# A two-block transformer on one core: four weight splits on another engine, and three steps added to the order of the second block

## The chip, the cores and the metric

The kernel runs on one core of a Trainium2 chip. The metric is the device time of one execution in microseconds (us), from the first to the last instruction with what lies around them; smaller is better. The engines are TensorE (PE in the rows; its weight loads are PEld), VectorE (DVE), ScalarE (ACT), GpSimd (POOL) and SyncE (SP, which issues most DMAs). Each engine works through its own queue in order; semaphores tie the queues together.

## What is computed

512 tokens of width 1024 go through two blocks, one layer each, all in 32-bit floats. The first block (a retention mixer, an RWKV mixer, cross-attention to 256 memory rows, a squared-ReLU MLP) is not touched by the change. The second block, which is, is this, cut to what matters:

```python
h = rmsnorm_2(x, norm_gain)
z = h @ w_in                                   # 1024 -> 4864
q, k, v, gate_a, u_in, v_in, gate_b, g_merge = split(z)
q = axial_rope(rmsnorm_2(q.reshape(B, S, 8, 64), q_gain), row_ang, col_ang)
k = axial_rope(rmsnorm_2(k.reshape(B, S, 2, 64), k_gain), row_ang, col_ang)
attn = block_attention(q, k, v) * silu(gate_a)   # 8 query heads, 2 key heads
y_a = attn @ w_proj_attn
u = gelu(u_in)
vv = layernorm(gelu(v_in), ln_v_gain, ln_v_bias)
v_mix = einsum('gij,bcjgd->bcigd', w_spatial, vv) + b_spatial
y_b = (u * v_mix * silu(gate_b)) @ w_proj_gmlp
g = sigmoid(g_merge + b_merge)
y = g[0] * y_a + g[1] * y_b
out = rmsnorm_2(x + y @ w_out, final_gain)
```

## The kernel before

**Weights.** All large weights lie in one stream of 189 units of 128 x 1024 floats, taken in order. A unit is loaded by SP into `raw`, rounded to the TensorE's reduced float form on ScalarE (`wh`, line 295), and the rest that the rounding lost is a subtraction `raw - wh` (`wl`, line 296). Each product of two matrices is then three TensorE products: high x high, high x low, low x high. Every fourth unit uses buffers of its own, named `rawx`, `whx`, `wlx` in the rows; the three others rotate over three buffers, so the cast of unit 148 can only start when the products with unit 144 are done. `self.lowpart(u)` says on which engine the subtraction of unit u runs: GpSimd where it is true, VectorE where not. Units are split three ahead of their use (`pump`).

**Units of the second block** (counted from the order of packing): 135 to 138 are q, 139 and 140 are k and v, 141 to 144 are u_in (one tile of 24 products each), 145 to 148 are v_in (one group of 96 products, which walks through all four units for each of the four row blocks), 149 to 156 the two gates, 157 to 172 the merge gates (16 tiles of 24 products), 173 to 188 the projections and the output.

**Order.** The order of the program is written out by hand with generators. `streams` runs a main generator one step at a time; each step issues about four large products. After each step it runs those side generators whose time has come: a `yield n` in a side generator means "go on n steps later". The TensorE's order is exactly the order of issue; the other engines' queues are ordered by the scheduler of the framework. Side generators here:
- `heads(b)` (lines 1229 to 1277): norm and rotation of q and k for row block b. The inverse root is `power` (line 372), a GpSimd operation; VectorE then scales (1244), multiplies by the rotation tables (1248), GpSimd adds the halves (1252, 1253), TensorE transposes, ScalarE and VectorE split the result (1261, 1262).
- `layer_norm(b)` (1298 to 1312): statistics on VectorE, `power` on GpSimd, scaling on VectorE (1307, 1308), gain and bias on GpSimd (1309, 1310).
- `attention()` (1365 to 1394): for each of 8 heads, four blocks of scores (`score`, into PSUM `tp`, softmax at lines 1109 to 1114) and four `turn`s (transposes of the probabilities into PSUM `ch`, split by ScalarE line 896 and VectorE line 897), then the products with the values: 8 products in two halves of four. They take the high and the low part of the turned probabilities in turn, so the second of them already needs the last VectorE split of the last `turn`.

Attention runs as a side stream between the products of the 16 merge-gate tiles. GELU (1194 to 1197) uses both ScalarE and VectorE. At the start of each tile ScalarE casts a unit (295) and evicts the tile before (1418), and GpSimd or VectorE makes a low part.

In the rows, `mm` and `cs` are the PSUM tiles of the main products; `s` and `t` are activations and temporaries. I number attention heads from 0, as the code does.

Of the kernel before, what the change touches and what calls it, by code (L numbers as in the profile page):

```python
# [212 lines left out]
class Ordered:  # L213


    def __init__(self, tc, eng):
        self.tc, self.eng, self.last = tc, eng, None
# [12 lines left out]
class Kern:  # L230
    def __init__(self, ctx, tc, A, out):
        self.tc, self.nc, self.A, self.out = tc, tc.nc, A, out
        self.T = Ordered(tc, tc.nc.tensor)
        pool = lambda name, **k: ctx.enter_context(tc.tile_pool(name=name, bufs=1, **k))
        self.cp = pool("cp")
        self.wp = pool("wp")
        self.tp = pool("tp")
        self.sp = pool("sp")
        self.sm = pool("sm")
        self.dp = pool("dp", space=bass.MemoryType.DRAM)  # L240
        self.nraw = self.nspl = 0
        self.raw, self.spl = {}, {}
        self.NU = A["wst"].shape[0]
        self.u = 0
        self.cnt = 0
        self.nh = 3
        self.lowpart = lambda u: u <= 3 or 55 <= u < 79 or 145 <= u
        self.wait = [40, 16]


# [948 lines left out]
    def second(self):  # L1199
# [32 lines left out]
        def heads(b):  # L1232
            x = qk[b]
            x3 = x.rearrange("p (h d) -> p h d", d=64)
            sq = self.tmp((P, 640), "t4", 2)
            for i in range(2):
                for k in range(2):
                    G.tensor_tensor(tab[i][k][:, b], tb[:, k, b], gq[i], op=ALU.mult)  # L1238
            SC.activation(sq, x, AF.Square)
            ss = self.small(10)  # L1240
            V.tensor_reduce(ss, sq.rearrange("p (h d) -> p h d", d=64), axis=AX.X, op=ALU.add)
            V.tensor_scalar(ss, ss, 1.0 / 64, 1e-6, op0=ALU.mult, op1=ALU.add)
            rn = self.power(ss, 10)
            V.tensor_tensor(x3, x3, rn.unsqueeze(2).broadcast_to([P, 10, 64]), op=ALU.mult)
            aa, bb = self.tmp((P, 640), "t4", 2), self.tmp((P, 640), "t4", 2)
            for i, (h0, h1) in enumerate(((0, 8), (8, 10))):
                for k, o in ((0, aa), (1, bb)):
                    V.tensor_tensor(o.rearrange("p (h d) -> p h d", d=64)[:, h0:h1], x3[:, h0:h1],
                                    tab[i][k][:, b].unsqueeze(1).broadcast_to([P, h1 - h0, 64]), op=ALU.mult)
            yield 3  # L1250
            v5 = lambda t: t.rearrange("p (g a f) -> p g a f", a=2, f=16)
            G.tensor_tensor(v5(x)[:, :, 0], v5(aa)[:, :, 0], v5(bb)[:, :, 1], op=ALU.subtract)
            G.tensor_tensor(v5(x)[:, :, 1], v5(aa)[:, :, 1], v5(bb)[:, :, 0], op=ALU.add)
            yield 15
            c = slice(b * 128, b * 128 + 128)
            tr = self.psum("tp", (P, 4, 128))
            for i in range(4):
                self.T.transpose(tr[:, i], x[:, i * 128:i * 128 + 128], self.ident)

            for q, (o, w) in zip(qt, both):  # L1260
                SC.copy(q[o, :, c], tr[o])
                V.tensor_tensor(q[w, :, c], tr[o], q[o, :, c].bitcast(F32), op=ALU.subtract)
            if b < NB - 1:
                return

            t = self.tmp((P, 2, 512), "t4", 2, F32R)
            kl.extend(t[:, r] for r in range(2))
            tr = self.psum("tp", (P, 4, 128))
            for i in range(NB):
                self.T.transpose(tr[:, i], qk[i][:, 512:640], self.ident)  # L1270
            tr = tr.rearrange("p a b -> p (a b)")
            for k, l, (o, w) in zip(kh, kl, both):
                SC.copy(k[o], tr[o])
                SC.copy(k[w], tr[o])
                V.tensor_tensor(l[o], tr[o], k[o].bitcast(F32), op=ALU.subtract)
                V.tensor_tensor(l[w], tr[o], k[o].bitcast(F32), op=ALU.subtract)
            self.flags.add("keys")
# [3 lines left out]
        def post(b, ps):  # L1281
            SC.copy(qk[b][:, 512:640], ps[:, 0:128])
            c = slice(b * 128, b * 128 + 64)
            self.psplit((vh[:, :, c], vl[:, :, c]), ps[:, 128:256].rearrange("p (r d) -> p r d", d=64))
            self.spawn(heads(b), 9 * b)
# [8 lines left out]
        def post(b, ps):  # L1294
            self.gelu2(ps, v2[:, b])
            self.spawn(layer_norm(b), 8)

        def layer_norm(b):
            v = v2[:, b]
            st = self.small(6)  # L1300
            V.bn_stats(st, v)
            mv = self.small(2)
            V.bn_aggr(mv, st)
            e = self.small(1)
            V.tensor_scalar(e, mv[:, 1:2], 0.25, 1e-6, op0=ALU.mult, op1=ALU.add)
            rs = self.power(e, 1)
            V.tensor_scalar(rs, rs, 0.5, None, op0=ALU.mult)
            V.tensor_scalar(v, v, mv[:, 0:1], rs, op0=ALU.subtract, op1=ALU.mult)
            G.tensor_tensor(v, v, lnt[:, 0], op=ALU.mult)
            G.tensor_tensor(v, v, lnt[:, 1], op=ALU.add)  # L1310
            return
            yield

        yield from self.quad(lambda k: h2[k], post, outer=True)

# [33 lines left out]
        def score(i):  # L1349
            p, r = i // 8, i // 4 % 2  # L1350
            c = slice(i % 4 * 128, i % 4 * 128 + 128)
            sc = self.psum("tp")
            self.T.matmul(sc, qt[r][:, p, c], kh[r], start=True, stop=False)
            self.T.matmul(sc, qt[r][:, p, c], kl[r], start=False, stop=True)
            pr[i] = self.softmax(sc, 512, 0.125)

        def turn(i):
            c = slice(i % 4 * 128, i % 4 * 128 + 128)
            if i % 4 == 0:
                pts[i // 4] = self.slab(13, [P, 4, 512], F32R), self.slab(17, [P, 4, 512], F32R)  # L1360
            pt = pts[i // 4]
            tr = self.psum("ch", (P, 4, 128))
            for m in range(4):
                self.T.transpose(tr[:, m], pr[i][:, m * 128:m * 128 + 128], self.ident)
            self.psplit((pt[0][:, :, c], pt[1][:, :, c]), tr)

        def attention():
            score(0)
            yield 1
            score(1)  # L1370
            yield 1
            for i in range(32):
                if i + 2 < 32:
                    score(i + 2)
                    yield 1
                turn(i)
                yield 1
                if i % 4 == 3:
                    hd = i // 4
                    o, w = both[hd % 2]  # L1380
                    yield 1
                    ps = self.psum("ch")
                    for m in range(4):
                        for k in range(2):
                            self.T.matmul(ps, vs(hd % 2, m), pts[hd][k][:, m], start=m + k == 0, stop=m + k == 4)
                        if m == 1:
                            yield 1
                    g = sga[o, hd // 2]
                    lo = self.tmp()
                    SC.activation(lo[o], ps[w], AF.Copy)  # L1390
                    V.tensor_tensor(lo[o], ps[o], lo[o], op=ALU.add)
                    V.scalar_tensor_tensor(g, lo[o], 0.5, g, op0=ALU.mult, op1=ALU.mult)
                    yield 1
            self.flags.add("attention")
# [16 lines left out]
        def post_b(j, ps):  # L1411
            o = th[2 + j // 4][:, j % 4]
            V.scalar_tensor_tensor(o, o, 1.0, ps, op0=ALU.add, op1=ALU.mult)

        self.spawn(attention(), 1)
        for j in range(16):
            ps = yield from self.tile_t(h2)
# [345 lines left out]
```

## Time and profile before

| | |
|---|---|
| time, median of 3 runs | 1276.71 us (1273.4 to 1277.31) |
| the profiled execution's own time | 1280.32 us |
| its span, first to last instruction | 1278.6 us |
| mean granted TensorE clock | 0.988 of full |
| TensorE busy | 1244.9 us, 97% of the span |
| VectorE busy | 654.0 us, 51% |
| ScalarE busy | 508.8 us, 40% |
| GpSimd busy | 473.0 us, 37% |

The busy time of TensorE comes from modelled ends of its matmuls, so a short wait can hide in it; the time from one matmul's start to the next one's start shows it better. Back-to-back products of 512 columns start about 0.23 us apart in this kernel. The granted clock is 1.0 at 2.4 GHz and 0.5 at 1.2 GHz.

### The profile page before, as it was taken

The page shows a single profiled execution, that of the slowest core. Times are in us where ns is not written, and L with a number is a line of the kernel's source. Part 1 is how long each engine was busy: PE and PEld are TensorE (multiplying, and loading weights), DVE is VectorE, ACT ScalarE, POOL GpSimd, SP SyncE. Part 2 cuts the span into 40 slices and gives each one's busy share as a digit, 9 for nine tenths or more (in the row PEclk, how much of TensorE's full clock was granted, in tenths as well). Part 3 has the DMA queues.
Part 4 walks back from the last instruction along what each step waited for, and adds up shares of the span by engine and source line. Part 5 has one row for each costly group of instructions (what it writes and reads, how often), then busy time and mean ns, then how long its engine had stood idle before and what let it go on. Part 6 is the DMA issues. An engine that isn't in the chain of part 4 may idle for free.

```text
span 1278.6 us, 17927 instructions
## 1 busy us (share of the span) xinstructions
PE 1244.9 (97%) x6976; PEld 1030.4 (81%) x6976; DVE 654.0 (51%) x1239; ACT 508.8 (40%) x919; POOL 473.0 (37%) x512
## 2 busy tenths in 40 slices
PE   7999989999999999999999999999999999999997
PEld 5777779887987888798888888888787878787886
DVE  4777334566784455434333333334667456564353
ACT  5434244232354444444332232234444445455232
POOL 4927571353200332344110111012526843233475
PEclk9999899999999999999999999999999999999999
DMA  5222423121345222223233333243232322121321
GB/s 202 74 67 85 114 51 86 50 67 34 117 138 178 78 86 66 83 81 118 88 95 98 99 99 97 92 119 97 93 103 63 116 83 66 50 67 50 115 83 67
DMA packets 52087, 115.47 MB, mean 90 GB/s; under 512 B 23169, under 2 KB 23809, under 8 KB 52002
## 3 DMA queue, kind: packets, MB, share of 16 engines
q1 hardware_dynamic: 47600, 113.73, 29.4%
q8 instruction: 55, 0.90, 0.3%
q10 hardware_dynamic: 4370, 0.59, 0.3%
q14 instruction: 30, 0.25, 0.1%
q0 software_dynamic: 32, 0.00, 0.0%
HBM read 110.90 MB, written 3.41 MB: 89 GB/s over the span
## 4 chain that ended last, share of the span: by engine, by line
PE 85%; DVE 5%; POOL 4%; ACT 3%; DMA 1%; issue 1%; ACTq 0%; POOLq 0%; DVEq 0%; SPq 0%
PE mm L221 40%; PE cs L221 33%; PE ch L221 8%; PE tp L221 4%; POOL o L1640 1%; POOL s L1642 1%; ACT wh L295 1%; DVE wl L296 1%; POOL s L1238 1%; ACT t L1112 0%; DVE t L1114 0%; DVE st L1718 0%; DVE s L221 0%; DVE s L897 0%; DMA s<-dm 0%
## 5 line engine op out<-in xcount | busy, mean ns | idle before, releaser
L221 PE MATMUL mm<-s,wh 128*128 128x512 f32 (+1 forms) x880 | 263.6, 379 | 2.3 <-DVE kt L775 2.1
L295 ACT CAST wh<-raw 128x1024 fp32r<-128x1024 f32 x151 | 158.7, 1051 | 259.7 <-PE mm L221 179.5
L221 PE MATMUL mm<-wh,s 128*128 128x512 f32 (+1 forms) x824 | 233.6, 352 | 3.8 <-DVE t L729 2.0
L296 DVE TENSOR_TENSOR wl<-raw,wh 128x1024 fp32r<-128x1024 f32 x99 | 122.9, 1241 | 156.3 <-ACT wh L295 155.9
L221 PEld LDWEIGHTS mm<-s,wh 128*128 128x128 f32 x880 | 159.6, 190 | 36.8 <-issue 6.2
L296 POOL TENSOR_TENSOR wl<-raw,wh 128x1024 fp32r<-128x1024 f32 x52 | 125.9, 2424 | 142.8 <-ACT wh L295 131.6
L221 PEld LDWEIGHTS mm<-wh,s 128*128 128x128 f32 x824 | 148.7, 194 | 24.3 <-issue 2.9
L221 PE MATMUL mm<-s,wl 128*128 128x512 f32 (+1 forms) x432 | 163.2, 378 | 1.0 <-DVE wl L221 1.0
L221 PE MATMUL cs<-s,wh 128*128 128x512 f32 (+1 forms) x544 | 154.8, 368 | 0.0
L221 PE MATMUL mm<-wl,s 128*128 128x512 f32 (+1 forms) x412 | 141.9, 344 | 2.1 <-POOL wl L296 1.6
L221 PE MATMUL cs<-wh,s 128*128 128x512 f32 (+1 forms) x440 | 142.2, 387 | 0.0
L1130 POOL TENSOR_TENSOR t<-t 128x512 f32<-128x512 f32 x32 | 49.9, 1558 | 217.0 <-ACT t L1129 217.0
L221 PEld LDWEIGHTS cs<-s,wh 128*128 128x128 f32 x544 | 98.2, 190 | 16.4 <-issue 0.2
L221 PE MATMUL cs<-s,wl 128*128 128x512 f32 (+1 forms) x272 | 99.9, 367 | 0.0
L221 PEld LDWEIGHTS cs<-wh,s 128*128 128x128 f32 x440 | 81.8, 188 | 16.4
L221 PEld LDWEIGHTS mm<-s,wl 128*128 128x128 f32 x432 | 82.4, 191 | 14.5 <-DVE wl L221 1.2
L296 POOL TENSOR_TENSOR wlx<-raw,whx 128x1024 fp32r<-128x1024 f32 x17 | 41.3, 2427 | 139.8 <-ACT whx L295 136.6
L221 PEld LDWEIGHTS mm<-wl,s 128*128 128x128 f32 x412 | 80.2, 195 | 11.7 <-POOL wl L296 2.0
L221 PE MATMUL cs<-wl,s 128*128 128x512 f32 (+1 forms) x220 | 85.1, 387 | 0.0
L351 DVE TENSOR_TENSOR s<-t,s 128x512 fp32r<-128x512 f32 x44 | 34.7, 790 | 65.2 <-ACT s L350 65.2
L221 PE MATMUL ch<-s,s 128*64 128x64 f32 (+3 forms) x504 | 62.5, 272 | 4.9 <-ACT s L1702 2.4
L295 ACT CAST whx<-raw 128x1024 fp32r<-128x1024 f32 x35 | 36.7, 1047 | 72.6 <-PE mm L221 53.0
(312 smaller groups left out, 2095.2 us busy)
## 6 DMA issues: line engine op xcount, KB each, us to landing
raw<-wst SPq DMA_DIRECT2D x189, 512.0 KB, 3.6
s<-x SPq DMA_DIRECT2D x8, 512.0 KB, 5.0
s<-rows SPq DMA_DIRECT2D x4, 512.0 KB, 4.0
out<-t SPq DMA_DIRECT2D x8, 256.0 KB, 2.2
t<-mem SPq DMA_DIRECT2D x2, 512.0 KB, 4.6
dm<-s ACTq DMA_DIRECT2D x8, 64.0 KB, 1.9
s<-dm SPq DMA_DIRECT2D x2, 256.0 KB, 4.1
s<-dm SPq DMA_DIRECT2D x8, 64.0 KB, 2.9
```

The costliest lines, as they stand in the source:

```text
L221: r = getattr(self.eng, name)(*a, **k)
L295: (SC or nc.scalar).copy(h, r)
L296: (E or (nc.gpsimd if self.lowpart(self.nspl) else nc.vector)).tensor_tensor(l, r, h.bitcast(F32), op=ALU.subtract)
L351: self.nc.vector.tensor_tensor(dst[1], src, dst[0].bitcast(F32), op=ALU.subtract)
L1130: nc.gpsimd.tensor_tensor(q, r, r, op=ALU.mult)
L1238: G.tensor_tensor(tab[i][k][:, b], tb[:, k, b], gq[i], op=ALU.mult)
L1640: G.tensor_tensor(tv, w[:, 0:k, s:s + 1].broadcast_to([P, k, n]), m[:, s:s + 1, s + 1:32].broadcast_to([P, k, n]), op=ALU.mult)
L1642: G.tensor_tensor(w[:, 0:k, s + 1:32], w[:, 0:k, s + 1:32], tv, op=ALU.add)
```

## The change

Three edits, all in the second block. Units 145 to 148 (v_in) get their low parts on VectorE instead of GpSimd. In `heads` and in `layer_norm` a `yield 2` stands between the power operation and the first instruction that uses its result, so that what follows is issued two steps later (in `heads` the transposes too, since the later waits count from there). In `attention` the pause between the last `turn` of a head and its value products is two steps instead of one.

```diff
-        self.lowpart = lambda u: u <= 3 or 55 <= u < 79 or 145 <= u
+        self.lowpart = lambda u: u <= 3 or 55 <= u < 79 or 149 <= u
...
             rn = self.power(ss, 10)
+            yield 2
             V.tensor_tensor(x3, x3, rn.unsqueeze(2).broadcast_to([P, 10, 64]), op=ALU.mult)
...
             rs = self.power(e, 1)
+            yield 2
             V.tensor_scalar(rs, rs, 0.5, None, op0=ALU.mult)
             V.tensor_scalar(v, v, mv[:, 0:1], rs, op0=ALU.subtract, op1=ALU.mult)
             G.tensor_tensor(v, v, lnt[:, 0], op=ALU.mult)
             G.tensor_tensor(v, v, lnt[:, 1], op=ALU.add)
-            return
-            yield
...
                 if i % 4 == 3:
                     hd = i // 4
                     o, w = both[hd % 2]
-                    yield 1
+                    yield 2
                     ps = self.psum("ch")
```

The instructions are the same but for their engine: VectorE has four more, GpSimd four fewer. Lines after 1243 have numbers one higher in the changed kernel up to `layer_norm`, and the old numbers again after it.

**ScalarE, around the cast of unit 148 (`wh_8737`), before.** Line 1261 splits turned q, 1239 squares for the norm, 1194 and 1196 are GELU of a tile of u_in.

```order
L1261 CAST s_1379_8169<-tp_8703 64x4x128
L1196 ACTIVATE t_8683<-t_8682 128x512
L1261 CAST s_1380_8170<-tp_8703 64x4x128
L1239 ACTIVATE t_1479_8750<-s_1378_8168 128x640
L295 CAST wh_8737<-raw_8631 128x1024
L1194 ACTIVATE t_8728<-mm_8694 128x512
```

The same place in the changed kernel:

```order
L1262 CAST s_1379_8169<-tp_8711 64x4x128
L295 CAST wh_8737<-raw_8631 128x1024
L1194 ACTIVATE t_8728<-mm_8692 128x512
L1262 CAST s_1380_8170<-tp_8711 64x4x128
L1239 ACTIVATE t_1479_8750<-s_1378_8168 128x640
L1196 ACTIVATE t_8729<-t_8728 128x512
```

The cast of unit 148 has moved ahead of a GELU step (1196), the second q split and the square; before, it stood behind all of them.

**VectorE, the same stretch, before.** 1244 scales q and k by the root, 1248 are the four rotation products, 1195 and 1197 belong to GELU.

```order
L1195 SCALAR_TENSOR_TENSOR t_8625<-t_8625,cs_8591 128x512
L1242 TENSOR_SCALAR sm_8652<-sm_8652 128x10
L1197 SCALAR_TENSOR_TENSOR s_1434_8521<-t_8626,cs_8591 128x512
L1244 TENSOR_TENSOR s_1378_8168<-s_1378_8168,sm_8655 128x640
L1248 TENSOR_TENSOR t_1463_8658<-s_1378_8168,s_1373_8149 128x512
L1248 TENSOR_TENSOR t_1464_8659<-s_1378_8168,s_1373_8149 128x512
L1248 TENSOR_TENSOR t_1463_8658<-s_1378_8168,s_1373_8149 128x128
L1248 TENSOR_TENSOR t_1464_8659<-s_1378_8168,s_1373_8149 128x128
L1195 SCALAR_TENSOR_TENSOR t_8682<-t_8682,cs_8637 128x512
L1262 TENSOR_TENSOR s_1379_8169<-tp_8703,s_1379_8169 64x4x128
L1197 SCALAR_TENSOR_TENSOR s_1434_8521<-t_8683,cs_8637 128x512
L1262 TENSOR_TENSOR s_1380_8170<-tp_8703,s_1380_8170 64x4x128
```

In the changed kernel (`wlx_8689` is the low part of unit 147, `wl_8738` that of unit 148):

```order
L296 TENSOR_TENSOR wlx_8689<-raw_8583,whx_8688 128x1024
L1195 SCALAR_TENSOR_TENSOR t_8680<-t_8680,cs_8637 128x512
L1245 TENSOR_TENSOR s_1378_8168<-s_1378_8168,sm_8655 128x640
L1197 SCALAR_TENSOR_TENSOR s_1434_8521<-t_8681,cs_8637 128x512
L1249 TENSOR_TENSOR t_1463_8666<-s_1378_8168,s_1373_8149 128x512
L1249 TENSOR_TENSOR t_1464_8667<-s_1378_8168,s_1373_8149 128x512
L1249 TENSOR_TENSOR t_1463_8666<-s_1378_8168,s_1373_8149 128x128
L1249 TENSOR_TENSOR t_1464_8667<-s_1378_8168,s_1373_8149 128x128
L1263 TENSOR_TENSOR s_1379_8169<-tp_8711,s_1379_8169 64x4x128
L296 TENSOR_TENSOR wl_8738<-raw_8631,wh_8737 128x1024
L1195 SCALAR_TENSOR_TENSOR t_8728<-t_8728,mm_8692 128x512
L1263 TENSOR_TENSOR s_1380_8170<-tp_8711,s_1380_8170 64x4x128
```

Two of the four new subtractions are seen here. The scaling (now 1245) has moved ahead of a GELU step, and the low part of unit 148 stands behind the four rotation products and one q split.

**TensorE, from the last turn of head 2 (the transposes with `ident`) to the first of its value products (`ch` from two `s`), before:**

```order
L221 MATMUL ch_9757<-ident,t_9689 128x128 x4
L221 MATMUL cs_9741<-s_1287_7754,wh_9490 128x512
L221 MATMUL cs_9741<-s_1285_7752,wl_9491 128x512
L221 MATMUL cs_9741<-s_1285_7752,wh_9490 128x512
L221 MATMUL cs_9741<-s_1287_7754,wh_9490 128x512
L221 MATMUL cs_9741<-s_1285_7752,wl_9491 128x512
L221 MATMUL cs_9741<-s_1285_7752,wh_9490 128x512
L221 MATMUL cs_9741<-s_1287_7754,wh_9490 128x512
L221 MATMUL cs_9741<-s_1285_7752,wl_9491 128x512
L221 MATMUL ch_9772<-s_1660_9669,s_1381_8171 128x512
```

In the changed kernel:

```order
L221 MATMUL ch_9765<-ident,t_9697 128x128 x4
L221 MATMUL cs_9723<-s_1286_7753,wh_9485 128x512
L221 MATMUL cs_9723<-s_1288_7755,wh_9485 128x512
L221 MATMUL cs_9723<-s_1286_7753,wl_9486 128x512
L221 MATMUL cs_9723<-s_1286_7753,wh_9485 128x512
...
L221 MATMUL cs_9723<-s_1286_7753,wl_9486 128x512
L221 MATMUL cs_9723<-s_1286_7753,wh_9485 128x512
L221 MATMUL cs_9723<-s_1288_7755,wh_9485 128x512
L221 MATMUL cs_9723<-s_1286_7753,wl_9486 128x512
L221 MATMUL ch_9792<-s_1660_9677,s_1381_8171 128x512
```

Eight main products stood between the turn and the value products; now there are twelve (four of them are the rows left out). The same holds for all eight heads: a head now takes 12 steps, 48 main products, which is two tiles, where it took 11 steps and 44 products (the last head, with no more scores to make, takes 40 where it took 36). So the tiles' starts fall at the same place of every head: counted from a head's value products, its successor's turns stand 12, 20, 28 and 36 products later and its value products 48 later, at the end of a tile. Before, this drifted by four products per head; only head 5's value products stood at the end of a tile (after 264 of the 384 products), and head 6's turns followed it 12, 20, 28 and 36 products later, its value products 44 later.

## Rows read from the trace of the kernel before

**Rows 1.** The page: busy time of an engine, share of the span, instructions.
```profile
PE 1244.9 (97%) x6976; PEld 1030.4 (81%) x6976; DVE 654.0 (51%) x1239; ACT 508.8 (40%) x919; POOL 473.0 (37%) x512
```

**Rows 2.** Busy time by stretch: each engine's, then granted clock, DMA share, GB/s.
```profile
1080.00:1100.00 20.00, 18.21 (x80) 14.27 (x79) 12.26 (x24) 8.23 (x17) 4.79 (x2) 0.91 0.19 53
1100.00:1180.00 80.00, 79.37 (x381) 63.65 (x380) 45.24 (x103) 42.50 (x81) 22.13 (x10) 1.00 0.20 60
...
1094.00:1098.00 4.00, 4.00 (x11) 3.14 (x12) 0.00 (x0) 0.00 (x0) 0.00 (x0) 0.57 0.37 123
```

**Rows 3.** Instructions in time (start, length, engine, line): TensorE at unit 148.
```profile
971.05 0.39 PE L221 MATMUL mm<-s,wl 128*128 128x512 f32 x1
...
975.39 0.40 PE L221 MATMUL mm<-wh,s 128*128 128x512 f32 x1
977.40 0.50 PE L221 MATMUL mm<-wl,s 128*128 128x512 f32 x1 [1.61 <-POOL wl L296]
```

**Rows 4.** The same view, other engines, on the way to unit 148's low part.
```profile
965.33 1.05 ACT L295 CAST whx<-raw 128x1024 fp32r<-128x1024 f32 x1 [0.52 <-PE cs L221]
...
966.47 2.39 POOL L296 TENSOR_TENSOR wlx<-raw,whx 128x1024 fp32r<-128x1024 f32 x1
966.54 3.00 DVE L1244 TENSOR_TENSOR s<-s,sm 128x640 f32<-128x640 f32 x1 [1.00 <-POOL sm L372]
...
969.58 1.70 DVE L1248 TENSOR_TENSOR t<-s,s 128x512 f32<-128x512 f32 x4
...
971.90 0.63 ACT L1196 ACTIVATE t<-t 128x512 f32<-128x512 f32 x1 [3.54 <-DVE t L1195]
...
973.87 1.03 ACT L295 CAST wh<-raw 128x1024 fp32r<-128x1024 f32 x1
...
974.98 2.36 POOL L296 TENSOR_TENSOR wl<-raw,wh 128x1024 fp32r<-128x1024 f32 x1 [1.91 <-ACT wh L295]
```

**Rows 5.** The page's costliest groups: a low part made on VectorE.
```profile
L296 DVE TENSOR_TENSOR wl<-raw,wh 128x1024 fp32r<-128x1024 f32 x99 | 122.9, 1241 | 156.3 <-ACT wh L295 155.9
```

**Rows 6.** Instructions in time: a VectorE low part beside GpSimd's rotation.
```profile
947.99 0.88 POOL L1253 TENSOR_TENSOR s<-t,t 128x320 f32<-128x320 f32 x1
948.20 1.75 DVE L296 TENSOR_TENSOR wlx<-raw,whx 128x1024 fp32r<-128x1024 f32 x1 [1.00 <-ACT whx L295]
```

**Rows 7.** Instructions in time, TensorE: value products of head 2.
```profile
1091.19 0.39 PE L221 MATMUL cs<-s,wl 128*128 128x512 f32 x1
1092.24 0.49 PE L221 MATMUL ch<-s,s 128*128 128x512 f32 x1 [0.66 <-ACT s L896]
1093.87 1.21 PE L221 MATMUL ch<-s,s 128*128 128x512 f32 x3 [1.13 <-DVE s L897]
...
1098.08 0.39 PE L221 MATMUL cs<-s,wh 128*128 128x512 f32 x1
```

**Rows 8.** The same time on the other engines.
```profile
1090.53 2.39 POOL L296 TENSOR_TENSOR wl<-raw,wh 128x1024 fp32r<-128x1024 f32 x1 [7.53 <-ACT wh L295]
...
1091.94 1.27 DVE L1114 TENSOR_SCALAR t<-t,sm 128x512 f32<-128x512 f32 x1
...
1093.13 0.68 DVE L897 TENSOR_TENSOR s<-ch,s 128x512 fp32r<-128x512 f32 x1
```

**Rows 9.** Instructions in time, TensorE: value products of head 4.
```profile
1127.41 0.40 PE L221 MATMUL ch<-s,s 128*128 128x512 f32 x1
1127.98 0.96 PE L221 MATMUL ch<-s,s 128*128 128x512 f32 x3 [0.17 <-DVE s L897]
```

**Rows 10.** Instructions in time: head 5's value products, and the end of head 6.
```profile
1143.55 1.09 PE L221 MATMUL ch<-s,s 128*128 128x512 f32 x4
...
1154.17 2.41 POOL L296 TENSOR_TENSOR wl<-raw,wh 128x1024 fp32r<-128x1024 f32 x1 [7.09 <-ACT wh L295]
...
1158.82 0.68 DVE L897 TENSOR_TENSOR s<-ch,s 128x512 fp32r<-128x512 f32 x1
...
1159.25 1.28 PE L221 MATMUL ch<-s,s 128*128 128x512 f32 x4
```

## The prediction

> **What bounds the kernel now.** I read the page first, then busy time by stretch, then the order of instructions in time, engine by engine. TensorE is busy for 97% of the span [rows 1], so nothing that only shortens work on another engine can show; a gain must be time in which TensorE stood still or ran at half clock. In the page the reader should compare the shares, and then look for stretches where TensorE falls short of their length. In the second block there are few: it stands still for 1.79 us of 1080 to 1100 and for 0.63 us of the 80 us after it [rows 2], and once in the v_in products, at unit 148 [rows 3]. Within 1094 to 1098 the mean granted clock is 0.57, so nearly all of it ran at the lower of the two levels, 1.2 GHz [rows 2]. That is all that the change can win, since it touches nothing ahead of 940 us and moves no TensorE work.
>
> Because a wait can hide in a modelled end, I size each by the time between two starts less the regular 0.23 us.
>
> **Unit 148 (the low parts on VectorE).** From 975.39 to 977.40 TensorE waits for unit 148's low part: 2.01 - 0.23 = 1.8 us [rows 3]. The rows tell how it came to be late. GpSimd makes unit 147's low part from 966.47 on; VectorE's scaling of k and q, issued just behind it, takes 3.00 us until 969.54, right after GpSimd ends; a GELU step on ScalarE then waits 3.54 us for VectorE, and behind it in ScalarE's queue stands the cast of unit 148 (973.87), though the buffer had been free since the last product with unit 144 at 971.4; the low part then takes 2.36 us on GpSimd [rows 3, 4].
>
> After the change nothing long of GpSimd's stands in the way of the scaling. The cast stands behind one q split only and can run from 971.4, when the buffer is free, to 972.4. On VectorE I add up what stands ahead of unit 148 from the end of unit 147's cast, 966.4 [rows 4]: that unit's low part 1.24 [rows 5], two GELU steps and one q split of 0.7 each (estimated from a split of that width, 0.68 [rows 8]), the scaling 0.8 (an estimate: 3.00 us less the 2.2 in which GpSimd was at work), the rotations 1.70 [rows 4]. That is 5.8 us, so VectorE is free at 972.2; the low part starts with the cast's end and is done at 972.4 + 1.24 = 973.6. TensorE asks for it at 975.39 + 0.23 = 975.6: 2.0 us to spare. Against this, GpSimd's two rotation sums of 0.88 us each start just then, when the rotations are done, and a VectorE low part that began beside such a sum took 1.75 us instead of 1.24 [rows 6]. If both sums hold it up it ends near 972.4 + 1.76 + 1.24 = 975.4, still 0.2 us early. If VectorE besides ran 1 us late, TensorE would wait 0.8. So the term lies between 1.0 and 1.8; I take **1.8**, as only two things together would cost any of it.
>
> The trace shows one engine standing until the other is done. The Trainium skill has this as a rule ("SBUF — State Buffer", section "Who interferes with whom"): a VectorE instruction with two SBUF inputs contends with a GpSimd one that reads SBUF, and the order of issue decides who stands still. The 3.00 us and the 1.75 us agree with it [rows 4, 6]. The rule speaks against this edit: it lets the power operation as well hold up a VectorE low part, which these rows don't show. If it does so for unit 147, by the 1.00 us that the scaling waited for that power, and the sums then hold up unit 148, both things do come together: the term is 1.0 by the rule, the sum 6.2 and the time 1270.5 instead of 1269.7.
>
> The four subtractions cost VectorE 4 x 1.24 = 5 us; it is idle for half of the span [rows 1], and what they delay (GELU, rotation of later row blocks) has several microseconds until TensorE asks. They take 4 x 2.4 us from GpSimd, which nobody waits for there but VectorE. Cost to the end: **0**. If that cover were gone, the q and k transposes would be late; they are issued eight products (1.8 us) later than before.
>
> **The steps after the power operation.** They add no instruction. They let VectorE take other work while GpSimd is at the power; that only shortens VectorE's waits. Bounds: nothing won beyond unit 148's term above, where the reordering is already counted, and at most 1 us lost if a transposed block came late. I take **0**.
>
> **The value products one step later.** What TensorE waits for there is the split of the last turn. The extra step puts four more main products, 4 x 0.23 = 0.92 us, between turn and value products; their work is not new, it only comes earlier. The terms:
> - Head 2, waits: 1091.19 to 1092.24 and 1092.24 to 1093.87, less 0.23 each: 0.82 + 1.40 = **2.2 us** [rows 7].
> - Head 2, clock: from 1093.87 to 1098.08 eleven products start, which at the regular 0.23 would be 2.53 us; they took 4.21, so **1.7 us** [rows 7]. The granted clock is 0.57 there and 1.0 in the stretch after it [rows 2]; the drop follows right on the two waits. It would go with them. Whether each execution has it I can't see from one; bounds 0 and 1.7.
> - Heads 3 to 7, waits: 0.63 us of idle [rows 2] is the lower bound. For head 4 the start-to-start time gives 0.57 - 0.23 = 0.34 where 0.17 is shown as idle [rows 9], so twice the idle, 1.3, is likelier; I take **1.3**.
>
> Do 0.92 us do? For head 2 alone they would not: its split ends at 1093.81, and with four more products TensorE would ask at about 1092.7. But the phase moves too. Head 2 was late because a tile's start fell into its last softmax: the unit cast there brought a GpSimd low part (1090.53 + 2.39 = 1092.92), and the last softmax scaling on VectorE took 1.27 us, until just after that, with the split behind it [rows 8]. After the change every head has the phase that heads 5 and 6 had before: value products at a tile's end, turns 12, 20, 28 and 36 products on. So the stretch from 1143.55 to 1159.25 is what each later head will look like, with four products more at its end [rows 10]. In it GpSimd's low part ends at 1156.6, well before the last split, and that split ends at 1158.82 + 0.68 = 1159.50, where TensorE asked for it at 1159.25 + 0.23 = 1159.48. With 0.92 us more that leaves 0.9 us to spare, seven times over. This is why I count all of the attention's waits as gone.
>
> At the other end, attention runs on for 32 products longer, into the first third of the next projection; 100 main products, 23 us, still lie between it and the projection that needs it. Cost: **0**.
>
> **Sum.** 1.8 + 2.2 + 1.7 + 1.3 = 7.0 us, against the profiled execution's 1280.32 us (span 1278.6): 1273.3 for such an execution. The median of the runs is 1276.71, 3.6 us lower, and I take the same difference off it: 1276.71 - 7.0 = **1269.7 us**.
>
> **Rivals.**
> 1. Only half of it shows. Unprofiled runs have no drop in the clock to win back, and either unit 148 is still late or the waits of heads 3 to 7 stay. For it: one profiled execution is all that shows the drop, and the sum on VectorE has 0.2 us to spare in its worse case. The gain is then 1.0 + 2.2 = 3.2 us or less: about 1273.5.
> 2. The change does nothing that can be told: TensorE's waits come back elsewhere in the stretch, as VectorE, held up by GpSimd, frees PSUM buffers later. For it: VectorE is at work for 45 and GpSimd for 22 of the 80 us after 1100. Against: TensorE stands still there for 0.63 us only, though that stretch has heads in four different phases [rows 2]. 1276 us.
> 3. Slower: the fixed phase is a bad one. If GpSimd's low part came to end beside the last softmax scaling of every head, each would lose head 2's 2.2 us less the 0.9 to spare, seven times: 9 us, against 7.0 won, so 1279; with a drop in the clock at each (7 x 1.7) up to 1291. In head 2 GpSimd was done 0.2 us before the split began (1092.92 and 1093.13), in the phase to come 2.2 us before it (1156.58 and 1158.82) [rows 8, 10]. It decides from the point where a cast comes some 2 us later than in rows 10, and the order of ScalarE's queue there gives no reason for that.
>
> **Chances.** Forecast (gains of 4 to 8 us) 0.74; rival 1 0.13; rival 2 0.09; rival 3 0.04. 0.3% of the median is 3.8 us, about what a measurement of this kernel can tell from no change. Forecast falls on the faster side; of rival 1 I put 0.03 there too: faster 0.77. Same 0.10 + 0.09 = 0.19, slower 0.04 (rival 3). The range: the lowest run of before less the whole sum is 1273.4 - 7.0 = 1266.4, and with a microsecond for waits sized too small 1265.4; upward it takes in most of rival 1, up to 1275.0. The forecast's own range is 1266.4 to 1272.7.
>
> **What would show it.** In the changed kernel: no wait of TensorE for a low part near 975 us, and the cast of unit 148 near 971; TensorE's start-to-start times at value products all near 0.23 us; a granted clock of 1.0 from 1080 to 1100; the attention's heads about 16 us apart. It is wrong if value products of all heads wait for line 897, if TensorE waits for a VectorE low part in v_in, or if a new half-clock stretch appears after 940 us.

## The result, and the profile after

The changed kernel takes 1271.07 us (median of 6 runs, 1267.94 to 1271.63); the kernel before, run beside it, 1277.6 us (6 runs, 1273.4 to 1280.13). The ratio is 0.9937 with a 95% interval of 0.9918 to 0.9955: faster, by 0.6%. The forecast was 1269.7 us (1265.4 to 1275.0). Of the 1.4 us between them, 0.9 is the median of before, 1276.71 in the first three runs and 1277.6 in six; the difference of the medians is 6.5 us where the sum said 7.0. The profiled execution of the changed kernel has a span of 1269.7 us, 8.9 below the 1278.6 of before.

The page's line of busy times, against [rows 1]:

```profile
PE 1241.8 (98%) x6976; PEld 1029.9 (81%) x6976; DVE 650.8 (51%) x1243; ACT 509.3 (40%) x919; POOL 463.1 (36%) x508
```

VectorE has four instructions more and GpSimd four fewer: the four low parts. Busy time by stretch, with the columns of [rows 2]:

```profile
1080.00:1100.00 20.00, 20.00 (x98) 16.41 (x97) 11.29 (x30) 10.92 (x23) 4.81 (x2) 1.00 0.22 67
1100.00:1180.00 80.00, 80.00 (x384) 65.48 (x384) 44.51 (x98) 42.01 (x79) 23.97 (x10) 1.00 0.20 61
1094.00:1098.00 4.00, 4.00 (x22) 3.26 (x21) 2.85 (x7) 1.68 (x4) 0.37 (x1) 1.00 0.44 131
```

TensorE is busy for the whole of both stretches, and the granted clock is 1.00 where it was 0.57. From 940 to 1262 us the list of TensorE's waits is empty. The instructions in time, first at unit 148 (to hold against [rows 3, 4]), then at head 2 (against [rows 7, 8]):

```profile
963.66 1.97 POOL L372 TENSOR_TENSOR sm<-sm,half 128x10 f32<-128x10 f32 x1 [4.54 <-DVE sm L1242]
964.99 1.23 DVE L296 TENSOR_TENSOR wlx<-raw,whx 128x1024 fp32r<-128x1024 f32 x1 [1.41 <-ACT whx L295]
966.73 0.82 DVE L1245 TENSOR_TENSOR s<-s,sm 128x640 f32<-128x640 f32 x1
969.82 1.05 ACT L295 CAST wh<-raw 128x1024 fp32r<-128x1024 f32 x1 [1.05 <-PE mm L221]
969.95 0.88 POOL L1253 TENSOR_TENSOR s<-t,t 128x320 f32<-128x320 f32 x1 [4.33 <-DVE t L1249]
970.79 0.88 POOL L1254 TENSOR_TENSOR s<-t,t 128x320 f32<-128x320 f32 x1
970.91 1.84 DVE L296 TENSOR_TENSOR wl<-raw,wh 128x1024 fp32r<-128x1024 f32 x1 [0.39 <-ACT wh L295]
973.98 0.39 PE L221 MATMUL mm<-wh,s 128*128 128x512 f32 x1
974.22 0.40 PE L221 MATMUL mm<-wl,s 128*128 128x512 f32 x1
...
1089.08 0.49 DVE L1114 TENSOR_SCALAR t<-t,sm 128x512 f32<-128x512 f32 x1
1089.48 0.69 DVE L897 TENSOR_TENSOR s<-ch,s 128x512 fp32r<-128x512 f32 x1
1090.60 0.40 PE L221 MATMUL cs<-s,wl 128*128 128x512 f32 x1
1090.83 1.10 PE L221 MATMUL ch<-s,s 128*128 128x512 f32 x4
```

At this point the execution runs 1.4 us ahead of before's. Unit 148's cast at 969.82 waits for TensorE alone, that is for its buffer. Its low part, 1.84 us beside GpSimd's two sums instead of 1.24, ends at 972.75; TensorE asks for it at 974.22. At head 2 the scaling takes 0.49 us instead of 1.27, and the split ends at 1090.17, 0.66 us before the value products start at 1090.83. The second of them is the first that needs the split, and it starts 0.24 us later, so 0.9 us are to spare. The same 0.66 stands at heads 1 to 6, and 0.87 and 0.92 at heads 0 and 7.

**Where the time came from.** Two executions differ ahead of the change as well, so I measure between the same products of each trace: the main products (TensorE's products into mm and cs tiles) counted in order, from the 4,201st (in the projection of k and v) over the 4,501st (behind the v_in products) to the 5,301st (behind attention). These are the three in the changed kernel:

```profile
936.96 0.28 PE L221 MATMUL mm<-wh,s 128*128 128x256 f32 x1
...
998.58 0.39 PE L221 MATMUL cs<-s,wh 128*128 128x512 f32 x1
...
1231.38 0.64 PE L221 MATMUL cs<-whx,s 128*128 128x512 f32 x2
```

In before they start at 938.35, 1001.93 and 1240.40. The times between them, for this pair and for all kernels told of below, from one trace each (us; "ahead" is from the first main product to the 4,201st):

| kernel | ahead | 4,201 to 4,501 | 4,501 to 5,301 |
|---|---|---|---|
| before | 933.1 | 63.58 | 238.47 |
| changed | 931.7 | 61.62 | 232.80 |
| lowparts | 927.5 | 61.68 | 236.93 |
| value_step | 931.4 | 63.46 | 232.80 |
| value_step_again | 931.2 | 63.56 | 232.80 |
| power_steps | 929.8 | 63.22 | 238.42 |
| no_power_steps | 928.7 | 61.68 | 232.80 |
| near_fixed | 930.2 | 61.62 | 232.88 |
| far_drift | 925.1 | 61.62 | 233.86 |
| phase_16 | 934.7 | 61.62 | 243.00 |
| phase_16_dve | 929.2 | 61.62 | 235.89 |
| unit147 | 935.0 | 61.62 | 232.80 |
| unit148 | 929.7 | 61.98 | 232.80 |
| fin_step | 928.1 | 61.62 | 232.80 |

The change won 1.96 us in the first stretch and 5.67 in the second, 7.6 together; 1.4 us more lie ahead of it, in code that is the same, and 0.2 are lost behind it, which gives the 8.9 but for rounding. Ahead the executions are up to 10 us apart, while the second block repeats to 0.1 us. The small experiments are therefore read from this table, and times only where they can tell.

### The profile page after: what moved, and what is told of

It is laid out like the page before. It is cut to its first block, busy times and chain, and to the rows that moved or that the text cites. A ratio compares the mean times of both kernels' runs of the same rounds, so it can differ in the third digit from the quotient of the medians.

```text
span 1269.7 us, 17926 instructions
## 1 busy us (share of the span) xinstructions
PE 1241.8 (98%) x6976; PEld 1029.9 (81%) x6976; DVE 650.8 (51%) x1243; ACT 509.3 (40%) x919; POOL 463.1 (36%) x508
## 4 chain that ended last, share of the span: by engine, by line
PE 87%; POOL 5%; DVE 3%; DMA 2%; ACT 2%; issue 1%; ACTq 0%; POOLq 0%; SPq 0%; DVEq 0%
PE mm L221 42%; PE cs L221 33%; PE ch L221 8%; PE tp L221 5%; POOL o L1640 2%; POOL s L1642 1%; POOL s L1238 1%; ACT wh L295 1%; DVE wl L296 1%; DMA dm<-s 0%; POOL t L980 0%; DMA t<-dm 0%; DVE s L221 0%; DVE st L1718 0%; DMA s<-dm 0%
## 5 line engine op out<-in xcount | busy, mean ns | idle before, releaser
L296 DVE TENSOR_TENSOR wl<-raw,wh 128x1024 fp32r<-128x1024 f32 x102 | 127.5, 1250 | 157.0 <-ACT wh L295 156.4
L296 POOL TENSOR_TENSOR wl<-raw,wh 128x1024 fp32r<-128x1024 f32 x49 | 118.8, 2427 | 127.8 <-ACT wh L295 127.7
```

The costliest lines, as they stand in the source:

```text
L296: (E or (nc.gpsimd if self.lowpart(self.nspl) else nc.vector)).tensor_tensor(l, r, h.bitcast(F32), op=ALU.subtract)
```

## The experiments

**The parts alone.** All four were timed beside the same runs of before, median 1276.62.

```
lowparts        before, and:  lowpart: 145 <= u -> 149 <= u
value_step      before, and:  ahead of the value products  yield 1 -> yield 2
power_steps     before, and:  yield 2 behind rn = self.power(ss, 10)
                              and behind rs = self.power(e, 1)
no_power_steps  changed, without these two  yield 2
```

lowparts: 

> The kernel before with the low parts of units 145 to 148 on VectorE and nothing else. Theory (the forecast's terms): unit 148's wait of 1.8 us goes, its cast stands near 970 to 971 us instead of 973.87; the attention is as before (head 2 waits 2.2 us and is followed by a half-clock stretch of some 3.4 us, heads 3 to 7 wait 1.3 to 1.9): 1277.6 - 1.8 = 1275.8 us. Rival: without the steps behind the power operation VectorE's scaling still stands waiting for GpSimd's power with a GELU step behind it, the cast comes 1 us or more later than 971, and TensorE still waits 0.5 to 1 us for unit 148: 1277 us.

value_step: 

> The kernel before with the value products one step later and nothing else. Theory: every wait at value products goes and so does the half-clock stretch behind head 2's; TensorE's start-to-start times there are 0.23 us, with 0.6 to 0.9 us to spare; unit 148's wait of 1.8 us stays: 1277.6 - 5.7 = 1271.9 us. Rival (the half-clock stretch is a chance of the one profiled execution, so that only waits can be won): 1277.6 - 4 = 1273.6 us, or less.

power_steps: 

> The kernel before with the two steps behind the power operation and nothing else. Theory (the forecast took 0 for them): VectorE's scaling still runs into GpSimd's low part of unit 147 and takes about 3 us, unit 148's wait stays near 1.8 us: 1277.6 us. Rival: with two steps between them a GELU step of VectorE goes ahead of the scaling, so ScalarE's GELU step and the cast behind it no longer wait 3.5 us; the cast of unit 148 comes near 970 to 971 us, and its wait falls below 0.5 us though all low parts are on GpSimd: 1276 us.

no_power_steps: 

> The changed kernel without the two steps behind the power operation (low parts on VectorE and later value products alone). Theory: the steps win nothing that TensorE sees, so no wait for unit 148 and none at value products: the changed kernel's 1271.1 us. Rival: the steps are what keeps VectorE from standing at the power operation; without them unit 148's low part ends 1 to 2 us later than the 972.75 us of the changed kernel and TensorE, which asks for it at 974.22, waits up to 0.8 us: 1271.9 us.

| kernel | median us | ratio to before, 95% interval |
|---|---|---|
| lowparts | 1275.66 | 0.9982 (0.9964 to 1.0001) |
| value_step | 1274.76 | 0.9984 (0.9964 to 1.0004) |
| power_steps | 1276.72 | 0.9996 (0.9978 to 1.0014) |
| no_power_steps | 1270.32 | 0.9957 (0.9941 to 0.9974) |

By their times alone only no_power_steps is told from before: the other three intervals hold 1. In the table of stretches the parts add up: the low parts alone win 1.9 us at unit 148, the later value products alone 5.67, and beside both the steps behind the power operation win 0.06, which is within the 0.1 us to which the stretch repeats. Alone they win 0.36 there, and the rows of power_steps tell why not more:

```profile
962.78 3.90 DVE L1249 TENSOR_TENSOR t<-s,s 128x512 f32<-128x512 f32 x4
...
962.99 2.74 POOL L296 TENSOR_TENSOR wlx<-raw,whx 128x1024 fp32r<-128x1024 f32 x1 [1.10 <-ACT whx L295]
...
967.32 0.63 ACT L1196 ACTIVATE t<-t 128x512 f32<-128x512 f32 x1 [3.78 <-DVE t L1195]
...
970.03 1.05 ACT L295 CAST wh<-raw 128x1024 fp32r<-128x1024 f32 x1
```

The scaling itself gets through, but now the rotations run into unit 147's low part, 3.90 us instead of 1.70 [rows 4], and the GELU step on ScalarE waits 3.78 us. This execution is 3.4 us ahead of before's at that point, so its cast at 970.03 is only 0.4 us earlier than the 973.87 of [rows 4]. The rivals for lowparts, power_steps and no_power_steps fell: TensorE has no wait at unit 148 in the first and the last, and 1.4 us of it in power_steps.

lowparts holds the finding on the clock. Its head 2 has the same two waits as before's, to 0.01 us:

```profile
1083.37 0.39 PE L221 MATMUL cs<-s,wl 128*128 128x512 f32 x1
1084.43 0.49 PE L221 MATMUL ch<-s,s 128*128 128x512 f32 x1 [0.67 <-ACT s L896]
1086.05 0.97 PE L221 MATMUL ch<-s,s 128*128 128x512 f32 x3 [1.13 <-DVE s L897]
```

But the stretch behind them, by busy time, is at full clock:

```profile
1086.05:1090.00 3.95, 3.95 (x17) 3.23 (x18) 0.45 (x1) 0.59 (x1) 0.00 (x0) 1.00 0.46 133
```

In power_steps the same stretch is mostly at 1.2 GHz, as in [rows 2]:

```profile
1090.50:1094.00 3.50, 3.50 (x11) 2.69 (x10) 0.00 (x0) 0.00 (x0) 0.00 (x0) 0.54 0.39 140
```

So the half-clock stretch came in two of the three executions that had these waits, and where it was absent the second stretch was 1.5 us shorter (236.93 against 238.42 and 238.47). Of the eleven executions without these two waits none has a half-clock stretch between 940 and 1260 us. That the waits bring it about is likely, but no run here isolates it.

value_step's time fits its trace badly: by the ratio it won 2.0 us where the trace has 5.7. It was timed again, in another set of runs.

> The kernel before with the value products one step later and nothing else, timed a second time, since the first timing gave 2 us where its trace shows 5.8 us less behind 940 us. Theory: the waits of 4.1 us are won in every execution and the half-clock stretch in some: 4.1 to 5.8 us below the kernel before, about 1271 to 1272.5 us. Rival: unprofiled executions lose it again, some 2 us below the kernel before, 1274.7 us.

This time 1272.44 against 1278.94 us, ratio 0.9947 (0.9926 to 0.9967): by the ratio 6.8 us. The trace is the same in the second block (232.80). About half of what lies between the two timings is the kernel before itself, whose median was 2.3 us lower in the first set. I put the rest down to the part ahead, but the executions that were timed without a trace don't show it; one set of runs doesn't settle 4 us here.

**Which unit matters.** Both take the changed kernel and leave one low part of the four on VectorE.

```
-149 <= u
+145 <= u and u != 147      unit147
+145 <= u and u != 148      unit148
```

unit147: 

> The changed kernel with only unit 147's low part on VectorE, those of units 145, 146 and 148 on GpSimd again (one look, for the trace). Theory: unit 147's low part on GpSimd is what holds VectorE up; with it moved the cast of unit 148 still stands near 970 us on the changed kernel's scale, its low part on GpSimd follows the two rotation sums and ends near 974.1 us, where TensorE asks at 974.2: a wait of 0 to 0.3 us. Rival (unit 148's own low part has to be on VectorE): TensorE waits 1 us or more there.

unit148: 

> The changed kernel with only unit 148's low part on VectorE, those of 145 to 147 on GpSimd again (one look, for the trace; the counterpart of unit147). Theory (unit 147's low part on GpSimd is the cause): VectorE is held up as before, the cast of unit 148 comes 2 to 4 us later than in the changed kernel, and with a low part of 1.24 instead of 2.36 us TensorE waits some 0.3 to 0.6 us there. Rival (the 1.1 us by which VectorE is faster are enough): no wait.

unit147, GpSimd and TensorE in time:

```profile
974.32 2.41 POOL L296 TENSOR_TENSOR wl<-raw,wh 128x1024 fp32r<-128x1024 f32 x1 [1.58 <-ACT wh L295]
...
977.27 0.40 PE L221 MATMUL mm<-wl,s 128*128 128x512 f32 x1
```

Unit 148's low part on GpSimd ends at 976.73, 0.54 us before TensorE asks: no wait, 61.62 as in the changed kernel. unit148:

```profile
969.70 1.05 ACT L295 CAST wh<-raw 128x1024 fp32r<-128x1024 f32 x1
970.78 1.23 DVE L296 TENSOR_TENSOR wl<-raw,wh 128x1024 fp32r<-128x1024 f32 x1
970.92 2.91 POOL L372 TENSOR_TENSOR sm<-sm,half 128x10 f32<-128x10 f32 x1 [2.76 <-DVE sm L1242]
971.61 0.40 PE L221 MATMUL mm<-wh,s 128*128 128x512 f32 x1
972.06 0.50 PE L221 MATMUL mm<-wl,s 128*128 128x512 f32 x1
```

This execution runs 2.4 us ahead of the changed kernel's, so its cast is 2.3 us later than there, and TensorE waits 0.45 - 0.23 = 0.2 us. Counted from power_steps, which has all four on GpSimd (63.22), unit 147's low part alone brings the whole 1.60 us (61.62), as the chain of rows had said. Unit 148's alone brings 1.24 (61.98): it doesn't touch the cause, but ends so much sooner that little of the wait is left. Those of units 145 and 146 bring nothing that shows.

**Distance or place.** The extra step does two things: four more products between last turn and value products, and a head period of 48 products, which puts each head at the same place in its tile. Two kernels have one of the two each, a third has both at another place.

```
near_fixed  changed, and: before the value products  yield 2 -> yield 1
                          at the head's end          yield 1 -> yield 2
far_drift   changed, without the  yield 1  at the head's end
phase_16    changed, and: self.spawn(attention(), 1) -> 5
```

near_fixed: 

> The changed kernel with the value products 8 main products behind the last turn again instead of 12, and the step put behind the head's end, so that the head period stays 48 products and every turn stays where it is. Theory (distance): the changed kernel has 0.66 us to spare at seven heads; less the 0.92 us of four products each of them waits 0.26 us, together 1.8 us and no half-clock stretch: 1271.1 + 1.8 = 1272.9 us. Rival 1 (the fixed phase alone does it): no waits, 1271.1 us. Rival 2 (only the distance counts): waits and half-clock stretch as in the kernel before, 1276 us.

far_drift: 

> The changed kernel without the step at a head's end, so that the value products keep 12 main products behind the last turn but the head period is 44 again and each head's place in its tile drifts as in the kernel before (one look, for the trace; the counterpart of near_fixed). Theory (the place decides, distance helps): head 2, whose last turn falls 4 products behind a tile's start, still waits 1.2 to 1.5 us as each head of phase_16 did; the other heads wait for nothing or 0.1 us; no half-clock stretch after 940 us, or one behind head 2: 1 to 3 us more than the changed kernel. Rival (12 products are enough by themselves): no wait anywhere, start-to-start as in the changed kernel.

phase_16: 

> The changed kernel with attention starting 16 main products (four steps) later, so that each head's last turn falls 4 products behind the start of a tile, where head 2 of the kernel before had it; period 48 and distance 12 stay. Theory (the forecast's third rival, the phase decides): head 2 of the kernel before asked 2.39 us too early; with 0.92 us more each of the seven heads waits about 1.5 us for the split, GpSimd's low part beside the last softmax scaling each time: 1271.1 + 10 = 1281 us, and up to 1291 us if a half-clock stretch follows each. Rival (head 2's wait was a one-off of drifting phases, 12 products are enough at any phase): no waits, 1271.1 us.

near_fixed took 1270.02 us, ratio 0.9934 (0.9913 to 0.9955), with no wait at any head: my theory fell, and its first rival held. The theory's 0.66 us ran to the first value product; counted to the second, which needs the split, it would have foreseen next to no wait itself. Head 2 in its trace:

```profile
1083.08 2.46 POOL L296 TENSOR_TENSOR wl<-raw,wh 128x1024 fp32r<-128x1024 f32 x1 [6.28 <-ACT wh L295]
...
1084.49 1.33 DVE L1114 TENSOR_SCALAR t<-t,sm 128x512 f32<-128x512 f32 x1
...
1087.00 0.68 DVE L897 TENSOR_TENSOR s<-ch,s 128x512 fp32r<-128x512 f32 x1
...
1087.98 1.08 PE L221 MATMUL ch<-s,s 128*128 128x512 f32 x4
```

A scaling is still held up by GpSimd, but one that stands a turn earlier; the last split stands ahead of the next scaling in VectorE's queue and ends 0.3 us before the value products with 8 main products only. The distance isn't needed at this place.

far_drift loses 1.1 us to the changed kernel (233.86), of the 4.1 to 5.7 that before loses. So the distance alone also does most of it. But the wait isn't where theory put it: it is 0.6 us at head 4, and 0.2 at a turn ahead of it. Head 2 has its turns behind the same main products as in before, and its last turn at the same place in a tile as the heads of phase_16, and it waits for nothing:

```profile
1078.89 2.39 POOL L296 TENSOR_TENSOR wl<-raw,wh 128x1024 fp32r<-128x1024 f32 x1 [7.03 <-ACT wh L295]
...
1080.17 0.69 DVE L897 TENSOR_TENSOR s<-ch,s 128x512 fp32r<-128x512 f32 x1 [0.68 <-ACT s L896]
...
1081.04 0.52 DVE L1114 TENSOR_SCALAR t<-t,sm 128x512 f32<-128x512 f32 x1
1082.12 1.11 PE L221 MATMUL ch<-s,s 128*128 128x512 f32 x4
```

Here the split stands ahead of the next scaling in VectorE's queue and ends at 1080.86, 1.26 us before the value products. In phase_16 it stands behind it, as in before's head 2 [rows 8]:

```profile
1115.01 2.42 POOL L296 TENSOR_TENSOR wl<-raw,wh 128x1024 fp32r<-128x1024 f32 x1 [7.41 <-ACT wh L295]
...
1116.42 1.30 DVE L1114 TENSOR_SCALAR t<-t,sm 128x512 f32<-128x512 f32 x1
1117.64 0.68 DVE L897 TENSOR_TENSOR s<-ch,s 128x512 fp32r<-128x512 f32 x1
...
1116.94 0.40 PE L221 MATMUL ch<-s,s 128*128 128x512 f32 x1
1118.38 0.96 PE L221 MATMUL ch<-s,s 128*128 128x512 f32 x3 [1.04 <-DVE s L897]
```

1.44 - 0.23 = 1.2 us are lost at this head (head 3), and 1.2 to 1.3 at six heads in a row (1 to 6); with 1.7 us at two turns of the last head and some tenths elsewhere it is 10.2 us more than in the changed kernel, where 10 were expected. phase_16 takes 1281.45 us beside 1278.94 for before, ratio 1.0016 (1.0000 to 1.0033): the same three edits, started four steps later, win nothing. No half-clock stretch follows any of the six waits.

**Is it GpSimd?** phase_16 with the low parts of the 16 merge units on VectorE:

```
-149 <= u
+149 <= u and not 157 <= u < 173
```

> phase_16 with the low parts of the 16 merge units (157 to 172) on VectorE instead of GpSimd (one look, for the trace). Theory (in the bad place GpSimd's low part holds up the last softmax scaling, 1.30 us instead of 0.49, and the split behind it): the scaling takes 0.49 us; VectorE's own low part of 1.24 us stands in its queue ahead of it, but begins with the cast's end, about 2.3 us before the scaling is asked for, so the six waits of 1.2 to 1.3 us shrink to 0.5 us or less each: 1273 to 1275 us. Rival (VectorE is simply full there): its low part takes the place of GpSimd's, waits of 1 us or more per head stay, 1281 us or more.

Its trace, first at head 3, then at head 6:

```profile
1105.53 1.22 DVE L296 TENSOR_TENSOR wl<-raw,wh 128x1024 fp32r<-128x1024 f32 x1
...
1106.73 0.68 DVE L897 TENSOR_TENSOR s<-ch,s 128x512 fp32r<-128x512 f32 x1
...
1107.86 0.49 DVE L1114 TENSOR_SCALAR t<-t,sm 128x512 f32<-128x512 f32 x1
...
1156.42 2.42 POOL L296 TENSOR_TENSOR wl<-raw,wh 128x1024 fp32r<-128x1024 f32 x1 [7.53 <-ACT wh L295]
...
1157.84 1.29 DVE L1114 TENSOR_SCALAR t<-t,sm 128x512 f32<-128x512 f32 x1
1159.06 0.68 DVE L897 TENSOR_TENSOR s<-ch,s 128x512 fp32r<-128x512 f32 x1
...
1158.31 0.40 PE L221 MATMUL ch<-s,s 128*128 128x512 f32 x1
1159.79 0.96 PE L221 MATMUL ch<-s,s 128*128 128x512 f32 x3 [1.08 <-DVE s L897]
```

Five of the six waits are gone, with 1.03 to 1.05 us between the split's end and the value products, and the split has moved ahead of the scaling. At head 6 the unit behind the merge units comes in, whose low part is still GpSimd's: there the scaling takes 1.29 us, the split stands behind it, and TensorE waits 1.25 us as in phase_16. The two turns of the last head keep their 1.6 us. So the waits go with GpSimd's low part. But two things changed at once, the scaling's length and the order, and the length alone doesn't suffice: by the rows it adds 1.30 - 0.49 = 0.8 us, so that an estimated 0.4 to 0.5 us of each wait would be left with the split behind a short scaling. No kernel here has one without the other.

**The lesson elsewhere.** fin_step puts a step between the power operation of the first block's final norm and VectorE's products with it, and takes one off the wait behind them.

```
 rs = self.power(c1, 1)
+yield 1
...
-yield 16
+yield 15
```

> The changed kernel with a step also between the first block's last power operation and VectorE's products with it (the final norm of each row block), one step taken off the wait behind them. It is the one wait of over 0.5 us behind 916 us that is left: TensorE stands 0.74 us at 923.69 us for a split that stands behind those products, which wait for GpSimd. Theory: the split goes ahead of the products and the wait goes, 0.7 to 0.9 us in the trace, too little for the timing: 1270.3 us against 1271.1. Rival: the products come later than the transposes that need them and TensorE waits as long elsewhere: 1271.1 us or 1 us more.

A miss: 1268.73 us, ratio to before 0.9941 (0.9917 to 0.9965), not to be told from the changed kernel's 0.9937, and TensorE still waits:

```profile
919.87 0.73 PE L221 MATMUL cs<-whx,s 128*128 128x512 f32 x2 [0.70 <-DVE s L897]
```

The split still stands behind those products on VectorE. No kernel here beats the changed one by more than these measurements can tell.

## Why the prediction was right, and where it was not

**Unit 148.** Taken at 1.8 us, measured 1.96. The cast came at 969.82, forecast 971.4 less the 1.4 us by which this execution is ahead; the low part was held up by the sums for 0.6 us of the allowed 1.76. That the four cost nothing on VectorE held too: TensorE has no other wait there. The case that followed the Trainium skill's rule ("SBUF — State Buffer", section "Who interferes with whom"), a power operation that holds up unit 147's low part, didn't happen: the low part began at 964.99 inside the power's 963.66 to 965.63 and took 1.23 us. On this point the trace goes against the rule. The rule's other half, that the order of issue decides, is seen in unit148, where the power was the second to start and took 2.91 us instead of 1.97.

**The steps after the power operation.** Taken at 0, measured 0.06 beside the low parts, no more than the stretch varies.

**The value products.** Head 2's waits were 2.2 us, as read from the rows. The clock term was sized as if sure, 1.7 us: it measures 1.5 and came in two of three executions. The waits of heads 3 to 7 were sized too small: 236.93 - 232.80 = 4.13, less head 2's 2.2, leaves 1.9 where I took 1.3; what I had left out are excesses of 0.1 to 0.2 us each. The total, 7.6 for 7.0, is the sum of these, with a clock term that is too large and waits that are too small. The medians moved by 6.5.

**The step that failed** is the answer to "Do 0.92 us do?", in its reasons and not in its sum. The spare time came out: 0.9 us forecast from the stretch of head 6 and four more products, 0.9 measured, both to the second value product. But I counted the place and the products together, and either does most of it alone. near_fixed has the place without the products, and wins 5.6 of the 5.7 us (232.88). far_drift has the products without the place, and wins 4.6 (233.86). "For head 2 alone they would not" was wrong: in far_drift head 2 has the turns of before and twelve products, and its split ends 1.26 us before the value products, where I had it end a microsecond too late. I had kept VectorE's queue in the order of the rows, with the split behind the scaling; there it stands ahead of it. The prediction didn't look at that order.

The third rival's mechanism, a fixed place that is bad, is real, but needs the start of attention four steps later. Its price of 9 us came near the 10.2 measured in part by luck: it is six heads and not seven, and 1.7 us lie at two turns of the last head, which the rival didn't have. Its sign, GpSimd's low part ending beside the last scaling, was the right thing to look for, but it isn't enough by itself: it costs where the split is queued behind that scaling (phase_16), not where it is queued ahead (far_drift).

**What would show it.** No wait near 975, the cast at 969.82, start-to-start times of 0.23 us at the value products, a clock of 1.00 from 1080 to 1100, and heads 16.6 us apart, all as named.

Open stay why the half-clock stretch follows head 2's waits in some executions only, what orders VectorE's queue one way in far_drift and the other in phase_16, and what made the two timings of value_step nearly 5 us apart.

## What to carry to other kernels

When a small stream runs beside a main loop, a period that is a multiple of the loop's makes one place repeat, the good one or the bad one (232.8 us against 243.0 here), so choose the place: ask which long GpSimd instruction runs when the stream's last VectorE step is due, and what is queued ahead of that step. Of several instructions moved between engines, follow the chain of waits to the one that blocks a queue; here one of four was enough for all of it, and it wasn't the one that TensorE waited for, which alone left a rest. Where executions differ by more than the effect, time the stretch between the same two instructions of both traces.

## What the runs showed of the hardware

**The part ahead.** The code ahead of the 4,201st main product, the same in all kernels but fin_step, took 925.1 to 935.0 us. Busy time of 140 to 300 us in far_drift, then in unit147, the two ends:

```profile
140.00:300.00 160.00, 149.59 (x1462) 129.65 (x1461) 79.88 (x182) 58.40 (x115) 74.10 (x137) 0.98 0.27 75
```

```profile
140.00:300.00 160.00, 150.14 (x1407) 130.85 (x1406) 71.77 (x166) 56.18 (x111) 68.47 (x131) 0.91 0.26 68
```

The mean granted clock is 0.98 in the one and 0.91 in the other: in the first, 55 products more start in the same time. Added up from the clock rows of the traces, TensorE ran at 1.2 GHz for 6.8 us of the part ahead in the first and for 30.7 us in the second; the other twelve traces lie between, and the more of it, the longer, with small exceptions, the part ahead took. Most of the 10 us between executions goes with that.

**A scaling with one tensor input stands too.** The softmax scaling (L1114, one tile in, one out) takes 0.49 us alone. Where it starts beside GpSimd's low part it ends 0.2 to 0.3 us behind it, so it takes 1.27 to 1.33 us in the lines above and up to 2.70 (far_drift, 1104.92 to 1107.62, beside a low part from 1104.94 to 1107.34). The prediction cited the Trainium skill's rule for instructions with two inputs only. The same section ("SBUF — State Buffer", "Who interferes with whom") says that a tensor_scalar can enter a mode that uses both ports and then contends; these rows agree on the standing, and don't show the mode.
